# Three 256-column matmuls per weight tile in the transposed products, instead of one of 512 and one of 256 columns in two addends

## The chip, the cores and the metric

The kernel runs on one core of a Trainium2 chip. The metric is the device time of one execution in microseconds, taken from the first to the last instruction and what little lies around them. TensorE (PE) multiplies, ScalarE (ACT), VectorE (DVE) and GpSimd (POOL) do the rest, and SyncE (SP) issues the DMAs. PE has two kinds of rows in the trace: its matmuls (PE) and its weight loads (PEld), which run beside them.

## The reference

One decoder layer on 256 tokens of 2048 features: a SwiGLU half-step, a mixer of two branches (latent attention, MLA, and a gated linear recurrence, HGRN), and a second SwiGLU half-step, each between two RMS norms.

```python
def swiglu(h, w_gate, w_up, w_down):
    return (jax.nn.silu(h @ w_gate) * (h @ w_up)) @ w_down
...
    x = x + MACARON_SCALE * rmsnorm(swiglu(rmsnorm(x, ...), w_gate, w_up, w_down), ...)
    proj = rmsnorm(x, ...) @ w_in        # c_q, c_kv, k_rope, hq, hf, hi, hg, gate_a, gate_b
    y_a = mla_branch(c_q, c_kv, k_rope, positions, ...)
    y_b = hgrn2_branch(hq, hf, hi, hg, ...)
    merged = sigmoid(gate_a) * y_a + sigmoid(gate_b) * y_b
    x = x + rmsnorm(merged @ w_out, ...)
    x = x + MACARON_SCALE * rmsnorm(swiglu(rmsnorm(x, ...), ...), ...)
```

Everything is float32. The width of the FFN is 5632.

## The kernel before

Every product takes both operands as sums of two float32r parts, hi and lo, and adds up three of the four partial products: hi by hi, hi by lo, lo by hi. The weights arrive by DMA in tiles of 128 x 1024 (`raw`, four buffers). ACT casts the tile to its hi part (`whi`, L95) and DVE subtracts it to get the lo part (`wlo`, L96), with four buffers each; both run about one product ahead of PE. The activation is kept split as [128, part, k-tile, 256 tokens] (`h1`, `after1`, `h2`, `oa`, `ob`, `cqT`, `ckvT`; in the trace `h`, `after` and so on).

There are two kinds of products. `gemm_n` has the activation as the loaded operand and the weights as the moving one (L126 to L128), 512 columns at a time, or 256 in the value products of MLA (`w_v`). `gemm_t` has the weights as the loaded operand, 128 columns at a time, and the activation as the moving one; its result is transposed, [column, token]. It is called 144 times: 80 times in the two FFNs (gate and up), 16 for the mixer's gates, 16 for HGRN's q and f, 16 for the two output projections, and 16 times over four k-tiles only, for MLA's q and k; all others run over 16 k-tiles. For each k-tile and each half j of 256 weight columns it issues two matmuls into the bank of that half: lo against the first part of the activation (256 columns, L114), and hi against both parts side by side (512 columns, L115); at the first k-tile the one of 512 comes first (L111, L112), since it has to open the whole bank. So a bank holds two addends of 256 columns. `Ops.total` adds them: ACT copies one out (L120) and DVE adds the other (L121); `pair_in` of HGRN has a `total` of its own (L630, L631) that also reorders. What follows (Silu, Sigmoid, the products with the gates) reads the sum from SBUF; in the two output projections POOL multiplies by the gates (L360, L375).

A product of the rotary key (L477 to L479) has weights of 64 columns and is written apart: three matmuls of 256 columns each, hi with the first part, hi with the second, lo with the first, into one region.

PSUM has two buffers `mm` of two banks each, which products take in turn, two of `tp` and two of `sp`. The order on each engine is the order in which the program is written, with some chains put ahead by `high_priority` (AHEAD); PE issues its matmuls strictly in that order. In HGRN the matmuls of a scan (L728, L741, L754) stand between those of the following pair's products.

Of the kernel before, what the change touches and what calls it, by code (L numbers as in the profile page):

```python
# [9 lines left out]
F32 = mybir.dt.float32  # L10
# [4 lines left out]
ALU = mybir.AluOpType  # L15
# [4 lines left out]
P = 128  # L20
# [17 lines left out]
# Where the next operand's transposes stand in program order, along the product that runs beside them (see gemm_n), and  # L38
# by how many instructions the rest of that operand's chain is put ahead; columns of the residual at a time.
# [9 lines left out]
def _two_pi_parts():  # L49
    """2 pi as a sum of four 12-bit numbers and a rest."""  # L50
    parts, rest = [], TWO_PI
    for _ in range(4):
        step = 2.0 ** (np.floor(np.log2(rest)) - 11)
        c = np.floor(rest / step) * step
        parts.append(float(c))
        rest -= c
    parts.append(float(np.float32(rest)))
    return parts


class Ops:
    """Pools and the pieces that the stages share."""
# [36 lines left out]
    def gemm_t(self, w, act, kt):  # L99
        """256 weight columns, result transposed: a bank for 128 columns, [column, token] in two addends."""  # L100
        nc = self.nc
        ps = self.mm.tile([P, 2, 512], F32, name="mm")
        for g in range(kt // 4):
            hi, lo = self.load_w(w[g])
            for i in range(4):
                k = g * 4 + i
                for j in range(2):
                    c = slice(i * 256 + j * P, i * 256 + (j + 1) * P)
                    both = act(k)
                    if k == 0:  # L110
                        nc.tensor.matmul(ps[:, j], hi[:, c], both, start=True, stop=False)  # L111
                        nc.tensor.matmul(ps[:, j, 0:T], lo[:, c], both[:, 0], start=False, stop=False)  # L112
                    else:
                        nc.tensor.matmul(ps[:, j, 0:T], lo[:, c], both[:, 0], start=False, stop=False)  # L114
                        nc.tensor.matmul(ps[:, j], hi[:, c], both, start=False, stop=k == kt - 1)  # L115
        return ps

    def total(self, out, ps):
        """The sum of gemm_t's two addends."""
        self.nc.scalar.copy(out=out, in_=ps[:, :, T:512])  # L120
        self.nc.vector.tensor_tensor(out=out, in0=out, in1=ps[:, :, 0:T], op=ALU.add)  # L121
# [8 lines left out]
    def gemm_n(self, w, act, kt, n=512, late=0, pool=None, own=0, hooks=()):  # L130
        """n weight columns, result [token, column], a bank for each half of the tokens.

        The first half of the tokens ends its last `late` k-tiles before the second half starts them. Their
        weights are in `pool`, but for the first `own` tiles. `hooks` are functions to call at points that run
        from -1 to 0 along the first half of the tokens, and from 0 to 1 along the second's last k-tiles."""
# [36 lines left out]
    def rstd_of(self, ssq, n, width, half=False):  # L172
        """ssq [P, n] sums of squares -> 1 / sqrt(mean + eps), or half of it."""
# [20 lines left out]
    def transposed(self, src, act, c, tt):  # L194
        """split(transpose(src)) into the k-tiles 4c.. of act."""
# [10 lines left out]
    def prenorm(self, x, ssq, wname, act, tt, ws=None):  # L206
        """act = split(transpose(x * rstd * w)) for half of the tokens."""
# [10 lines left out]
    def weighted(self, ps, c, z, wname):  # L218
        """z = y * w, a quarter of the columns."""
# [3 lines left out]
    def residual(self, x, z, rstd, done):  # L223
        """x += rstd * z, some of the columns at a time."""
# [6 lines left out]
    def closing(self, w, act, kt, late, own, pool, post, half, x_src, x_dst, nxt):  # L231
        """The last product of a stage, its norm, the residual, and the next stage's operand.

        Returns the hooks of the next product, which end the operand."""
# [33 lines left out]
def layer_kernel(ctx, tc, a, out):  # L268
# [9 lines left out]
    def ffn(n, act, fp, x_src, x_dst, nxt, hooks=()):  # L278
# [3 lines left out]
        # the first columns by halves of the tokens  # L282
# [8 lines left out]
        for c in range((FF - FF_N) // 256):  # L291
            pg = ops.gemm_t(wg[c], act, KD)
            sg = fp.tile([P, 2, T], F32, name="sg", bufs=2)
            ops.total(sg, pg)
            S.activation(out=sg, in_=sg, func=AF.Silu)
            pu = ops.gemm_t(wu[c], act, KD)
            su = ops.small.tile([P, 2, T], F32, name="m", bufs=2)
            ops.total(su, pu)
            V.tensor_tensor(out=sg, in0=sg, in1=su, op=ALU.mult)
# [39 lines left out]
    def gate_a(c):  # L339
        pg = ops.gemm_t(a["w_ga"][c], h, KD)  # L340
        g = ga[:, 2 * c:2 * c + 2]
        ops.total(g, pg)
        S.activation(out=g, in_=g, func=AF.Sigmoid)

    def gate_b(c):
        pg = ops.gemm_t(a["w_gb"][c], h, KD)
        t = gbp.tile([P, 2, T], F32, name="gb", bufs=3)
        ops.total(t, pg)
        S.activation(out=t, in_=t, func=AF.Sigmoid)
# [5 lines left out]
    for c in range(8):  # L355
        py = ops.gemm_t(a["mla_w_o"][c], lambda k: oa[:, :, k, :], KD)
        m = ops.small.tile([P, 2, T], F32, name="m", bufs=2)
        ops.total(m, py)
        g = ga[:, 2 * c:2 * c + 2]
        G.tensor_tensor(out=g, in0=g, in1=m, op=ALU.mult)  # L360
# [5 lines left out]
    with tc.tile_pool(name="mg", bufs=1, side="right", reuse_waits="tile") as mgp:  # L366
        mg = mgp.tile([P, 2, KD, T], F32R, name="mg")
        for c in range(8):
# [5 lines left out]
            ops.total(m, py)  # L374
            G.tensor_tensor(out=m, in0=m, in1=gts[c], op=ALU.mult)  # L375
# [15 lines left out]
def rope_tables(ops, pool):  # L391
    """cos and sin of positions * inv_freq as [token, half of the tokens, HALF]."""
# [17 lines left out]
    # whole turns off: their number in parts of ten bits, so that each product with a part of 2 pi is exact  # L410
# [22 lines left out]
def mla(ops, mp, c_q, hm, h, oa, gate):  # L433
# [16 lines left out]
    def rope(dst, src, tt, n):  # L450
        """src [P, n, 64] -> dst, rotated."""
# [18 lines left out]
    # k_rope: product transposed, back to [token, dim], rotated, transposed, for the even and the odd  # L470
    # head of a pair in its half of the partitions, with zeros in the other
# [40 lines left out]
    def heads_in(pair, step):  # L512
        qn = mp.tile([P, 2, T], F32, name="qn", bufs=3)
        ops.total(qn, ops.gemm_t(a["w_q_nope"][pair], cq, KL))
        step()
        kn = mp.tile([P, 2, T], F32, name="kn", bufs=3)
        ops.total(kn, ops.gemm_t(a["w_k_nope"][pair], ckv, KL))
# [381 lines left out]
```

## Time and profile before

| what | us |
|---|---|
| median of three runs | 2564.39 (2564.3 to 2566.51) |
| span of the profiled execution | 2564.2 |
| PE busy | 2521.4 |
| PE weight loads busy | 2147.1 |
| DVE busy | 1477.7 |
| ACT busy | 1186.9 |
| POOL busy | 181.1 |

The span of the profiled execution is 0.2 us under the median; what lies around it is less than the runs differ by. PE's rows overlap each other, so the distance between the starts of two matmuls in a row tells more than the duration of one. In the 40 slices of the page PE is at 9 tenths or more but for the first and the last, the granted clock is at 9 or more throughout, and the DMA engines are busy between 4 and 8 tenths.

### The profile page before, as it was taken

To read this page: it belongs to the slowest core of one execution; us is meant where nothing else is said; L and a number is where in the kernel's file an instruction comes from. 1 tells how busy PE (TensorE), PEld (TensorE's weight loads), DVE (VectorE), ACT (ScalarE), POOL (GpSimd) and SP (SyncE) were. 2 spreads that over 40 slices of the span, in tenths; PEclk is the share of its full clock that TensorE was granted. 3 is DMA by queue.
4 is the path that set the end of the run, shared out by engine and by line. 5 is a ranking of instruction groups with operands and counts; after the bars stand their busy time and mean duration, and the time that the engine had idled before them with its cause. 6 is when DMAs were issued, how large, how long until landed. Compare 5 with 4: busy or idle time off the path is not lost.

```text
span 2564.2 us, 33907 instructions
## 1 busy us (share of the span) xinstructions
PE 2521.4 (98%) x13316; PEld 2147.1 (84%) x13316; DVE 1477.7 (58%) x1732; ACT 1186.9 (46%) x1552; POOL 181.1 (7%) x181
## 2 busy tenths in 40 slices
PE   8999999999999999999999999999999999999998
PEld 6888888888878898888888888888788888888887
DVE  5555555544466666556777776555655555554444
ACT  5444444434344556444444444444544444443433
POOL 0000000000000100111323231120000000000000
PEclk9999999999999999999999999999999999999999
DMA  7555555556686444555545444567755555555655
GB/s 255 174 188 189 188 183 190 188 188 199 201 271 188 162 140 148 188 181 181 165 163 169 161 157 158 188 205 242 231 175 188 187 186 188 189 189 188 197 195 184
DMA packets 137248, 481.13 MB, mean 188 GB/s; under 512 B 15616, under 2 KB 16000, under 8 KB 136320
## 3 DMA queue, kind: packets, MB, share of 16 engines
q1 hardware_dynamic: 137088, 478.97, 57.3%
q8 instruction: 104, 1.70, 0.3%
q14 instruction: 56, 0.46, 0.1%
HBM read 472.61 MB, written 6.29 MB: 187 GB/s over the span
## 4 chain that ended last, share of the span: by engine, by line
PE 93%; DVE 3%; POOL 1%; issue 1%; DMA 1%; ACT 1%; SPq 0%; POOLq 0%; DVEq 0%; ACTq 0%
PE mm L115 34%; PE mm L114 18%; PE mm L126 11%; PE mm L127 11%; PE mm L128 11%; PE mm L111 2%; PE mm L112 1%; POOL suf L706 1%; PE tp L198 0%; DVE sT L711 0%; PE sp L534 0%; PE sp L533 0%; DVE wlo L96 0%; PE sp L728 0%; PE tp L565 0%
## 5 line engine op out<-in xcount | busy, mean ns | idle before, releaser
L96 DVE TENSOR_TENSOR wlo<-raw,whi 128x1024 fp32r<-128x1024 f32 x826 | 1024.8, 1243 | 763.5 <-ACT whi L95 762.3
L95 ACT CAST whi<-raw 128x1024 fp32r<-128x1024 f32 x826 | 865.7, 1050 | 891.2 <-PE mm L115 425.3
L115 PE MATMUL mm<-h,whi 128*128 128x512 f32 x2400 | 846.0, 393 | 0.0
L114 PE MATMUL mm<-h,wlo 128*128 128x256 f32 x2400 | 678.1, 283 | 0.0
L115 PEld LDWEIGHTS mm<-h,whi 128*128 128x128 f32 x2400 | 450.7, 188 | 100.7
L114 PEld LDWEIGHTS mm<-h,wlo 128*128 128x128 f32 x2400 | 451.2, 188 | 3.8
L115 PE MATMUL mm<-after,whi 128*128 128x512 f32 x960 | 340.1, 394 | 0.0
L114 PE MATMUL mm<-after,wlo 128*128 128x256 f32 x960 | 273.1, 284 | 0.0
L127 PE MATMUL mm<-wlo,at 128*128 128x512 f32 x664 | 262.0, 395 | 0.0
L126 PE MATMUL mm<-whi,at 128*128 128x512 f32 x664 | 262.0, 395 | 0.0
L128 PE MATMUL mm<-whi,at 128*128 128x512 f32 x664 | 261.7, 395 | 0.0
L115 PEld LDWEIGHTS mm<-after,whi 128*128 128x128 f32 x960 | 180.4, 188 | 38.9
L114 PEld LDWEIGHTS mm<-after,wlo 128*128 128x128 f32 x960 | 180.6, 188 | 1.2
L126 PEld LDWEIGHTS mm<-whi,at 128*128 128x128 f32 x664 | 125.1, 188 | 29.2
L128 PEld LDWEIGHTS mm<-whi,at 128*128 128x128 f32 x664 | 125.1, 188 | 29.2
L127 PEld LDWEIGHTS mm<-wlo,at 128*128 128x128 f32 x664 | 125.1, 188 | 29.2
L178 POOL TENSOR_TENSOR rs<-ms,mhalf 128x1 f32<-128x1 f32 x16 | 9.7, 605 | 1633.3 <-DVE ms L176 1633.3
L126 PE MATMUL mm<-whi,after 128*128 128x512 f32 x304 | 120.9, 398 | 1.2 <-ACT after L164 1.2
L128 PE MATMUL mm<-whi,after 128*128 128x512 f32 x304 | 120.1, 395 | 0.0
L127 PE MATMUL mm<-wlo,after 128*128 128x512 f32 x304 | 120.0, 395 | 0.0
L115 PE MATMUL mm<-oa,whi 128*128 128x512 f32 x240 | 84.6, 393 | 0.0
L115 PE MATMUL mm<-ob,whi 128*128 128x512 f32 x240 | 84.6, 393 | 0.0
(276 smaller groups left out, 2860.9 us busy)
## 6 DMA issues: line engine op xcount, KB each, us to landing
raw<-in_ffn_w_gate SPq DMA_DIRECT2D x176, 512.0 KB, 4.3
raw<-in_ffn_w_up SPq DMA_DIRECT2D x176, 512.0 KB, 3.5
raw<-in_ffn_w_down SPq DMA_DIRECT2D x176, 512.0 KB, 4.3
raw<-in_w_ga SPq DMA_DIRECT2D x32, 512.0 KB, 3.4
raw<-in_mla_w_o SPq DMA_DIRECT2D x32, 512.0 KB, 3.6
raw<-in_w_hq SPq DMA_DIRECT2D x32, 512.0 KB, 3.6
raw<-in_w_hf SPq DMA_DIRECT2D x32, 512.0 KB, 3.5
raw<-in_w_hi SPq DMA_DIRECT2D x32, 512.0 KB, 3.5
```

The costliest lines, as they stand in the source:

```text
L95: nc.scalar.copy(out=hi, in_=raw)
L96: nc.vector.tensor_tensor(out=lo, in0=raw, in1=hi.bitcast(F32), op=ALU.subtract)
L111: nc.tensor.matmul(ps[:, j], hi[:, c], both, start=True, stop=False)
L112: nc.tensor.matmul(ps[:, j, 0:T], lo[:, c], both[:, 0], start=False, stop=False)
L114: nc.tensor.matmul(ps[:, j, 0:T], lo[:, c], both[:, 0], start=False, stop=False)
L115: nc.tensor.matmul(ps[:, j], hi[:, c], both, start=False, stop=k == kt - 1)
L126: nc.tensor.matmul(o, both[:, 0, r], hi[:, c], start=k == 0, stop=False)
L127: nc.tensor.matmul(o, both[:, 0, r], lo[:, c], start=False, stop=False)
L128: nc.tensor.matmul(o, both[:, 1, r], hi[:, c], start=False, stop=k == kt - 1)
L178: self.nc.gpsimd.tensor_tensor(out=r, in0=ms, in1=self.mhalf[:, 0:n], op=ALU.pow)
L706: G.tensor_tensor(out=part(suf, n, True), in0=part(suf, n, True), in1=ends(pre, n, False), op=ALU.mult)
```

## The change

`gemm_t` issues three matmuls of 256 columns for each k-tile and half, all into the first 256 columns of the bank: hi with the first part of the activation, hi with the second part, lo with the first part. The first opens the region at the first k-tile, the last closes it at the last. The result is complete in PSUM, and `total` is gone. Silu and Sigmoid on ACT and the multiplies on DVE read PSUM; MLA's q and k are copied out by ACT; in the two output projections the multiply by the gate moves from POOL to DVE, with its operand from PSUM; HGRN's q and f are read in the order that `total` made. Comments and docstrings are taken out, so that line numbers move.

```diff
     def gemm_t(self, w, act, kt):
-        ps = self.mm.tile([P, 2, 512], F32, name="mm")
+        banks = self.mm.tile([P, 2, 512], F32, name="mm")
+        ps = banks[:, :, 0:T]
...
                     both = act(k)
-                    if k == 0:
-                        nc.tensor.matmul(ps[:, j], hi[:, c], both, start=True, stop=False)
-                        nc.tensor.matmul(ps[:, j, 0:T], lo[:, c], both[:, 0], start=False, stop=False)
-                    else:
-                        nc.tensor.matmul(ps[:, j, 0:T], lo[:, c], both[:, 0], start=False, stop=False)
-                        nc.tensor.matmul(ps[:, j], hi[:, c], both, start=False, stop=k == kt - 1)
+                    nc.tensor.matmul(ps[:, j], hi[:, c], both[:, 0], start=k == 0, stop=False)
+                    nc.tensor.matmul(ps[:, j], hi[:, c], both[:, 1], start=False, stop=False)
+                    nc.tensor.matmul(ps[:, j], lo[:, c], both[:, 0], start=False, stop=k == kt - 1)
         return ps
-
-    def total(self, out, ps):
-        self.nc.scalar.copy(out=out, in_=ps[:, :, T:512])
-        self.nc.vector.tensor_tensor(out=out, in0=out, in1=ps[:, :, 0:T], op=ALU.add)
...
             sg = fp.tile([P, 2, T], F32, name="sg", bufs=2)
-            ops.total(sg, pg)
-            S.activation(out=sg, in_=sg, func=AF.Silu)
+            S.activation(out=sg, in_=pg, func=AF.Silu)
             pu = ops.gemm_t(wu[c], act, KD)
-            su = ops.small.tile([P, 2, T], F32, name="m", bufs=2)
-            ops.total(su, pu)
-            V.tensor_tensor(out=sg, in0=sg, in1=su, op=ALU.mult)
+            V.tensor_tensor(out=sg, in0=sg, in1=pu, op=ALU.mult)
...
         py = ops.gemm_t(a["mla_w_o"][c], lambda k: oa[:, :, k, :], KD)
-        m = ops.small.tile([P, 2, T], F32, name="m", bufs=2)
-        ops.total(m, py)
         g = ga[:, 2 * c:2 * c + 2]
-        G.tensor_tensor(out=g, in0=g, in1=m, op=ALU.mult)
+        V.tensor_tensor(out=g, in0=g, in1=py, op=ALU.mult)
...
         qn = mp.tile([P, 2, T], F32, name="qn", bufs=3)
-        ops.total(qn, ops.gemm_t(a["w_q_nope"][pair], cq, KL))
+        S.copy(out=qn, in_=ops.gemm_t(a["w_q_nope"][pair], cq, KL))
...
-        total(q, ops.gemm_t(a["w_hq"][pr], h, KD))
-        S.activation(out=sg, in_=q, func=AF.Sigmoid)
-        V.tensor_tensor(out=q, in0=q, in1=sg, op=ALU.mult)
+        pq = ordered(ops.gemm_t(a["w_hq"][pr], h, KD))
+        S.activation(out=sg, in_=pq, func=AF.Sigmoid)
+        V.tensor_tensor(out=q, in0=sg, in1=pq, op=ALU.mult)
```

The gates, HGRN's f and the second output projection change in the same way.

On PE, at the turn from one FFN product to the next (`mm` with its number is the product's PSUM buffer, `h1` the activation, `whi` and `wlo` the two parts of a weight tile), before:

```order
L114 MATMUL mm_804<-h1_86,wlo_874 128x256
L115 MATMUL mm_804<-h1_86,whi_873 128x512
L111 MATMUL mm_899<-h1_86,whi_902 128x512
L112 MATMUL mm_899<-h1_86,wlo_903 128x256
L111 MATMUL mm_899<-h1_86,whi_902 128x512
L112 MATMUL mm_899<-h1_86,wlo_903 128x256
L114 MATMUL mm_899<-h1_86,wlo_903 128x256
L115 MATMUL mm_899<-h1_86,whi_902 128x512
```

The same place on PE in the changed kernel:

```order
L111 MATMUL mm_893<-h1_86,whi_986 128x256
L112 MATMUL mm_893<-h1_86,whi_986 128x256
L113 MATMUL mm_893<-h1_86,wlo_987 128x256
L111 MATMUL mm_1017<-h1_86,whi_1020 128x256
L112 MATMUL mm_1017<-h1_86,whi_1020 128x256
L113 MATMUL mm_1017<-h1_86,wlo_1021 128x256
```

Each pair of rows has become three, and the special order of the first k-tile is gone; between other work the triples stand where the pairs stood, within a matmul or two.

On DVE, over one gate and one up product of an FFN (`sg` is the gate, `m` the sum of the up product, `at` the split result), before:

```order
L165 TENSOR_TENSOR at<-sg,at 128x512
L96 TENSOR_TENSOR wlo<-raw,whi 128x1024 x3
L121 TENSOR_TENSOR sg<-sg,mm 128x512
L96 TENSOR_TENSOR wlo<-raw,whi 128x1024 x4
L121 TENSOR_TENSOR m<-m,mm 128x512
L299 TENSOR_TENSOR sg<-sg,m 128x512
L96 TENSOR_TENSOR wlo<-raw,whi 128x1024
L165 TENSOR_TENSOR at<-sg,at 128x512
```

The same stretch of DVE in the changed kernel:

```order
L158 TENSOR_TENSOR at<-sg,at 128x512
L96 TENSOR_TENSOR wlo<-raw,whi 128x1024 x7
L289 TENSOR_TENSOR sg<-sg,mm 128x512
L96 TENSOR_TENSOR wlo<-raw,whi 128x1024
L158 TENSOR_TENSOR at<-sg,at 128x512
```

The add for the gate has gone from between the splits of weights, and the multiply (L299, now L289; L165 is now L158) takes its second operand from PSUM.

## Rows read from the trace of the kernel before

**Rows 1.** The page's part 1: engine, busy us, share of the span, instructions.

```profile
PE 2521.4 (98%) x13316; PEld 2147.1 (84%) x13316; DVE 1477.7 (58%) x1732; ACT 1186.9 (46%) x1552; POOL 181.1 (7%) x181
```

**Rows 2.** The page's part 4: the chain that ended last.

```profile
PE 93%; DVE 3%; POOL 1%; issue 1%; DMA 1%; ACT 1%; SPq 0%; POOLq 0%; DVEq 0%; ACTq 0%
PE mm L115 34%; PE mm L114 18%; PE mm L126 11%; PE mm L127 11%; PE mm L128 11%; PE mm L111 2%; PE mm L112 1%; POOL suf L706 1%; PE tp L198 0%; DVE sT L711 0%; PE sp L534 0%; PE sp L533 0%; DVE wlo L96 0%; PE sp L728 0%; PE tp L565 0%
```

**Rows 3.** By stage: us, busy (count) of PE, PEld, DVE, ACT, POOL; clock; DMA.

```profile
70.00:515.00 445.00, 445.00 (x2537) 389.63 (x2536) 243.91 (x236) 207.27 (x237) 0.00 (x0) 1.00 0.58 187
515.00:750.00 235.00, 235.00 (x1014) 190.65 (x1013) 111.23 (x97) 95.28 (x102) 0.00 (x0) 1.00 0.65 210
...
1205.00:1560.00 355.00, 342.83 (x1852) 289.62 (x1851) 259.60 (x406) 167.31 (x300) 108.43 (x108) 1.00 0.49 157
```

**Rows 4.** Timeline of PE, steady FFN product: start us, duration us, engine, line, operation.

```profile
505.26 0.28 PE L114 MATMUL mm<-h,wlo 128*128 128x256 f32 x1
505.38 0.39 PE L115 MATMUL mm<-h,whi 128*128 128x512 f32 x1
505.60 0.28 PE L114 MATMUL mm<-h,wlo 128*128 128x256 f32 x1
505.72 0.40 PE L115 MATMUL mm<-h,whi 128*128 128x512 f32 x1
...
511.22 0.28 PE L114 MATMUL mm<-h,wlo 128*128 128x256 f32 x1
```

**Rows 5.** Timeline of PE, a value product of MLA.

```profile
873.79 0.28 PE L126 MATMUL mm<-whi,ckvT 128*128 128x256 f32 x1
873.90 0.28 PE L127 MATMUL mm<-wlo,ckvT 128*128 128x256 f32 x1
...
876.40 0.28 PE L128 MATMUL mm<-whi,ckvT 128*128 128x256 f32 x1
```

**Rows 6.** Timeline of PE, the product of the rotary key.

```profile
817.06 0.28 PE L477 MATMUL mm<-after,whi 128*64 128x256 f32 x1
817.18 0.28 PE L478 MATMUL mm<-after,whi 128*64 128x256 f32 x1
...
818.46 0.28 PE L477 MATMUL mm<-after,whi 128*64 128x256 f32 x1
```

**Rows 7.** Timeline of PE, the head of an FFN product.

```profile
504.09 0.28 PE L112 MATMUL mm<-h,wlo 128*128 128x256 f32 x1
504.21 0.28 PE L114 MATMUL mm<-h,wlo 128*128 128x256 f32 x1
504.32 0.39 PE L115 MATMUL mm<-h,whi 128*128 128x512 f32 x1
```

**Rows 8.** Timeline of PE, end of the last down product.

```profile
2549.74 0.39 PE L126 MATMUL mm<-wpair,at 128*128 128x512 f32 x1
...
2552.46 0.39 PE L126 MATMUL mm<-wpair,at 128*128 128x512 f32 x1
```

**Rows 9.** Weight loads by shape: line, operation, shapes, count, busy us, mean ns.

```profile
L115 PEld LDWEIGHTS mm<-h,whi 128*128 128x128 f32 x2400 | 450.7, 188 | 100.7
L477 PEld LDWEIGHTS mm<-after,whi 128*64 128x64 f32 x16 | 2.1, 134 | 0.0
```

**Rows 10.** Lines L120 and L121: count, duration in ns (least, median, most).

```profile
L120 ACT COPY m<-mm x56: 587/587/588, 88.1 to 2310.9; 128x512 f32<-128x512 f32 x56
L121 DVE TENSOR_TENSOR m<-m,mm x56: 686/687/690, 88.7 to 2311.6; 128x512 f32<-128x512 f32 x56
```

**Rows 11.** Timelines of PE and DVE in HGRN.

```profile
1216.92 0.68 PE L741 MATMUL sp<-A,B 128*128 128x128 f32 x4 [1.41 <-DVE B L737]
...
1228.12 0.69 DVE L631 TENSOR_TENSOR q<-q,mm 128x512 f32<-128x512 f32 x1 [0.52 <-ACT q L630]
```

**Rows 12.** Timeline of DVE, and the chain, at HGRN's last pair.

```profile
1548.71 0.68 DVE L121 TENSOR_TENSOR gb<-gb,mm 128x512 f32<-128x512 f32 x1
...
1549.39 1.05 ACT whi L95
```

More of the change, by code (lines that the diff above doesn't have):

```diff
@@ L341, in gate_a @@
         g = ga[:, 2 * c:2 * c + 2]
-        ops.total(g, pg)
-        S.activation(out=g, in_=g, func=AF.Sigmoid)
+        S.activation(out=g, in_=pg, func=AF.Sigmoid)
     def gate_b(c):
@@ L347, in gate_b @@
         t = gbp.tile([P, 2, T], F32, name="gb", bufs=3)
-        ops.total(t, pg)
-        S.activation(out=t, in_=t, func=AF.Sigmoid)
+        S.activation(out=t, in_=pg, func=AF.Sigmoid)
         return t
@@ L373, in layer_kernel @@
             cs = slice(2 * c, 2 * c + 2)
-            ops.total(m, py)
-            G.tensor_tensor(out=m, in0=m, in1=gts[c], op=ALU.mult)
+            V.tensor_tensor(out=m, in0=gts[c], in1=py, op=ALU.mult)
             G.tensor_tensor(out=m, in0=m, in1=ga[:, cs], op=ALU.add)
@@ L513, in heads_in @@
         qn = mp.tile([P, 2, T], F32, name="qn", bufs=3)
-        ops.total(qn, ops.gemm_t(a["w_q_nope"][pair], cq, KL))
+        S.copy(out=qn, in_=ops.gemm_t(a["w_q_nope"][pair], cq, KL))
         step()
         kn = mp.tile([P, 2, T], F32, name="kn", bufs=3)
-        ops.total(kn, ops.gemm_t(a["w_k_nope"][pair], ckv, KL))
+        S.copy(out=kn, in_=ops.gemm_t(a["w_k_nope"][pair], ckv, KL))
         step()
@@ L625, in pair_in, with ordered @@
         tmp = lambda: gp.tile([P, 2, 2, P], F32, name="tmp", bufs=2)
-        def total(t, ps):
-            o = t.rearrange("p t j n -> p j t n")
-            half = lambda s: ps[:, :, s * T:(s + 1) * T].rearrange("p j (t n) -> p j t n", n=P)
-            S.copy(out=o, in_=half(1))
-            V.tensor_tensor(out=o, in0=o, in1=half(0), op=ALU.add)
+        def ordered(ps):
+            return ps.rearrange("p j (t n) -> p t j n", n=P)
         q = gp.tile([P, 2, 2, P], F32, name="q", bufs=2)
         sg = tmp()
-        total(q, ops.gemm_t(a["w_hq"][pr], h, KD))
-        S.activation(out=sg, in_=q, func=AF.Sigmoid)
-        V.tensor_tensor(out=q, in0=q, in1=sg, op=ALU.mult)
+        pq = ordered(ops.gemm_t(a["w_hq"][pr], h, KD))
+        S.activation(out=sg, in_=pq, func=AF.Sigmoid)
+        V.tensor_tensor(out=q, in0=sg, in1=pq, op=ALU.mult)
         f = gp.tile([P, 2, 2, P], F32, name="f", bufs=2)
@@ L640, in pair_in @@
         step(1)
-        total(sf, ops.gemm_t(a["w_hf"][pr], h, KD))
+        pf = ordered(ops.gemm_t(a["w_hf"][pr], h, KD))
         step(1)
-        S.activation(out=sf, in_=sf, func=AF.Sigmoid)
+        S.activation(out=sf, in_=pf, func=AF.Sigmoid)
         for j in range(2):
```

## Prediction

> **What bounds the kernel now.** I read the page first: PE is busy 98% of the span, DVE 58%, ACT 46% [rows 1]. The chain that ended last is PE for 93%, and gemm_t's four lines (L111, L112, L114, L115) are 55% of the span on it; DVE, POOL and ACT together are 5% [rows 2]. The table by stage then says where PE waits at all: in the first FFN's transposed products PE is busy 445.00 of 445 us, in the down product 235.00 of 235, and only in the HGRN stage does it stand still, for 355 - 342.83 = 12 us. The granted clock is 1.00, the 2.4 GHz level, in each [rows 3]. So the end is set by how fast PE passes through its own queue of matmuls; time is lost or won per matmul slot, which I take as the distance from one start to the next. A row's own duration (0.28 us for 256 columns) is of no use for that, since matmuls overlap.
>
> In the steady part of an FFN product the pattern is one 256-column slot of 0.12 us and one 512-column slot of 0.22 us or a little more. From 505.26 to 511.22 there are 17 such pairs, so a pair takes 5.96 / 17 = 0.3506 us [rows 4]. A product over 16 k-tiles has 32 pairs and there are 128 of them; 16 products over 4 k-tiles have 8 pairs each: 4096 + 128 = 4224 pairs. They take 4224 x 0.3506 = 1481 us of 2564.2.
>
> **The change part by part.** *The matmuls.* Each pair becomes three slots of 256 columns. The columns are the same 768, so nothing is gained or lost by counting columns; what counts is what a third matmul, with a third weight load, adds. Break-even is a mean slot of 0.3506 / 3 = 0.1169 us. No row of before shows three full-width 256-column matmuls in a row with the activation moving, so I bound the slot from both sides.
>
> Below: the value products (w_v) stream 256 columns against 128-column loads, 23 slots from 873.79 to 876.40, 2.61 / 23 = 0.1135 us each [rows 5]. There the roles are swapped: the weights move and the activation is loaded. Three such slots are 0.3405, 0.0101 less than a pair, or 4224 x 0.0101 = 43 us less. In the middle: k_rope is already written as the changed code is, same moving operand and same order of hi, hi, lo, but loads only 64 weight columns; 12 slots from 817.06 to 818.46 are 1.40 / 12 = 0.1167 us [rows 6]. Three are 0.3500, 4224 x 0.0006 = 2.5 us less. Above: L114 is itself the third matmul of the changed triple, unaltered: lo against the first half of the activation, 256 columns, 128-column loads on both sides, into the same region. Its slot is 0.12 us [rows 4] (of the 17 in that stretch 15 read 0.12 and two 0.13, rounded as they are; I take 0.1200); three such are 0.3600, 0.0094 more than a pair, 4224 x 0.0094 = +39.7 us. I take this row, because it is the nearest: operands, widths and role are those of the new code, and the other two rows each differ in what is loaded. Against it stands one place: at the head of each product L112 is followed by L114, two 256-column matmuls in a row, and the two slots are 504.32 - 504.09 = 0.23 us together, 0.115 each [rows 7]. That is two slots in a transition; I keep it for the rivals.
>
> What would make the third slot cost something: a 512-column slot is 0.3506 - 0.1200 = 0.2306 us, a 256-column slot 0.1200; a straight line through the two gives 0.0094 us per matmul beside its columns. One matmul more per pair is then the same +39.7 us. But a second line, through the slots where the weights move, does not have that part: 512 columns take 2.72 / 12 = 0.2267 us from 2549.74 to 2552.46 [rows 8], which is twice 0.1135 to within 0.0003. So the price of a matmul as such is between 0 and 0.0094 us here, and which of the two holds decides the case.
>
> The Trainium skill (TensorE: Matmul & The Clock Gate, section Back-to-back issue gap) speaks against the change too: at the high clock it gives N / 2.4 ns plus a fixed 2.5 ns for each matmul. By that price the sum would be 4224 x 2.5 ns = +10.6 us, an estimate from that page. No row here shows a price of that size; the two lines give nothing and nearly four times as much.
>
> *The weight loads.* 4224 more. A load is recorded as 188 ns for 128 columns and 134 ns for 64 [rows 9], so 64 columns cost 54 ns and 128 about 108 ns of streaming (an estimate from these rows), the rest being latency. 108 ns fits under a slot of 113 to 120 ns, and the loads run beside the matmul before them; w_v shows exactly this load at that pace. They cost nothing by themselves, but they leave 5 to 12 ns of slack where a 512-column matmul left over 110; if that cover is gone, each slot is set by its load.
>
> *The totals.* 128 copies on ACT of 0.587 us fall away (75 us), and on DVE 144 adds of 0.687 us, while 16 multiplies by the gates come to DVE from POOL [rows 10]: 128 x 0.687 = 88 us less. None of it is on the path in the FFN stages, where PE waits for nobody [rows 3]. In HGRN the PE stalls belong to the scan: PE is held until 1216.92 by DVE's L737, and the chain there is POOL and DVE work on suf and f; the adds of the totals lie outside, at 1228.12 [rows 11]. The last pair has an add at 1548.71 just ahead of a step of the scan, 0.68 us, but ACT's cast of 1549.39 to 1550.44 ends after it on the chain [rows 12]. I take 0 of the 0.7 us. PSUM regions are released earlier by the two operations, and no PE row in the steady part waits for one: 0.
>
> *Order and waits.* On DVE the gate's add no longer stands between the splits, and the multiply by the up product waits for PE directly instead of for ACT's copy. Queued behind it are the next splits of weights (L96), which already stood behind the add that waited for the same product; they run one product ahead (4 buffers), and no PE time hangs on it in these stages. 0. With slower slots the scan's stalls shrink a little, since the products between its steps last longer: in each of 8 pairs some 5 us of such products by 2.7%, about -1 us in all.
>
> Sum: 2564.2 + 39.7 - 1 = 2602.9. The span of the profiled execution is 0.2 us under the median of 2564.39, so I predict **2603** us. Its own range is 2596 to 2609 (slots of 0.1195 to 0.1205: 33 to 46 us).
>
> **The rivals.** *The weight load sets the pace and the stream closes up (faster).* In w_v the slots are at 0.11 us from the first one on and stay at 0.1135. If the triples do the same, whichever operand is loaded, PE gains 43 us and gives about 1 us back in the scan's stalls: 2522. For it: the only long stream of this exact shape in the trace does so, and the pair at a product's head is at 0.115 [rows 5, 7]. Against it: L114, with the loads of the new code, never shows it in the steady part. It decides below a mean slot of 0.1169 us.
>
> *Splitting the 512 costs nothing (no change).* The halves take what the whole took, and the mean slot stays near k_rope's 0.1167: 2564.2 - 2.5 - 0.5 = 2561, between 2557 and 2568 for slots of 0.1164 to 0.1172 [rows 6]. For it: same operands and order. Against it: half the load.
>
> *A small fixed price per matmul.* The two straight lines give 0 and 0.0094 us; a price of a quarter of the second, 0.0025, adds 4224 x 0.0025 = 10.6 us: 2575. The page named above gives the same. Neither line supports the middle, so the chance is small.
>
> **How the numbers follow.** Forecast 0.42, closed-up stream 0.25, nothing 0.25, small price 0.08. The likeliest time is 2603. To leave out no more than 2 in 10 the range must reach both 2522 and 2603 with their spreads: 2520 to 2609. What a measurement here can tell from no change is about 0.2%, 5.1 us. Faster by more than that: the closed-up stream and 0.07 of the case of no change, 0.32. Within: 0.17. Slower: 0.42 + 0.08 + 0.01 = 0.51.
>
> **What would show it.** In the profile after, take the starts of the three lines in a steady FFN product: a triple of 0.360 us confirms the forecast, 0.350 the case of no change, 0.340 the closed-up stream; times 4224 it must give the difference in the end to a few us. The FFN stages should carry 80/144 of the products and a like share of the difference, PE's busy share there should stay whole, and ACT and DVE should lose some 75 and 88 us. If the triple is 0.350 and the time still moves by more than 5 us, then the consumers matter and my reading of what is off the path is wrong; the HGRN stage, with its 12 us of standing still, is where that would show. If PE begins to wait for splits or for PSUM in the FFN stages, the part on order is wrong.

## The result, and the profile after

The changed kernel takes 2590.34 us (median of 4, 2589.65 to 2594.64), the kernel before, run beside it, 2565.45 us (2564.30 to 2568.03): 24.9 us more, ratio 1.0099, interval [1.0084, 1.0113]. It is slower, as forecast; the forecast of 2603 us was 13 us too high.

The profiled execution of the changed kernel took 2594.64 us, its span 2592.9 us. Part 1 of its page (engine, busy us, share, instructions), and the chain that ended last:

```profile
PE 2549.6 (98%) x17540; PEld 2362.0 (91%) x17540; DVE 1386.2 (53%) x1604; ACT 1120.6 (43%) x1424; POOL 144.5 (6%) x165
```

```profile
PE 94%; DVE 3%; POOL 1%; issue 1%; DMA 1%; ACT 0%; SPq 0%; POOLq 0%; DVEq 0%; ACTq 0%
```

Beside [rows 1, 2]: 4224 matmuls and as many loads more, DVE 91 us less, ACT 66 and POOL 37 us less, and PE on the path as before. The weight loads went from 84% of the span to 91%. The same three stretches of time as in [rows 3], of which the second and third stage now begin later, by 12 and 17 us (us; busy us and count of PE, PEld, DVE, ACT, POOL; clock; DMA share; GB/s):

```profile
70.00:515.00 445.00, 445.00 (x3711) 445.00 (x3710) 214.04 (x193) 181.38 (x193) 0.00 (x0) 1.00 0.55 183
515.00:750.00 235.00, 235.00 (x1059) 192.51 (x1058) 109.91 (x94) 94.63 (x100) 0.00 (x0) 1.00 0.62 204
1205.00:1560.00 355.00, 342.37 (x2212) 308.41 (x2211) 246.64 (x376) 157.26 (x267) 102.61 (x109) 1.00 0.50 161
```

PE still waits for nobody in the FFN; in HGRN it stands still 355 - 342.37 = 12.6 us, against 12.2 before. What changed is that in the first stage a weight load is now under way at every moment: 445.00 of 445 us, where it was 389.63. No new wait was made and none removed. The time went into the slots. In the steady part of the first FFN (start us, duration us, engine, line, operation):

```profile
505.03 0.28 PE L113 MATMUL mm<-h,wlo 128*128 128x256 f32 x1
505.15 0.29 PE L111 MATMUL mm<-h,whi 128*128 128x256 f32 x1
505.27 0.28 PE L112 MATMUL mm<-h,whi 128*128 128x256 f32 x1
...
506.59 0.29 PE L111 MATMUL mm<-h,whi 128*128 128x256 f32 x1
```

From the first to the last are 13 slots, 1.56 / 13 = 0.1200 us each: every matmul of the triple goes at the pace that only L114 had in [rows 4]. A finer measure of the mean is how many matmuls pass in 300 us of a pure FFN product. Of the kernel before, and of the changed one (stretch, length, busy us of PE and count, clock, DMA share, GB/s):

```profile
100.00:400.00 300.00, 300.00 (x1711) 1.00 0.58 188
1950.00:2250.00 300.00, 300.00 (x1712) 1.00 0.58 187
```

```profile
100.00:400.00 300.00, 300.00 (x2502) 1.00 0.55 183
1950.00:2250.00 300.00, 300.00 (x2530) 1.00 0.57 186
```

Before, a pair takes 600 / 1711 = 0.3507 us in the first FFN and the same in the second. After, a triple takes 900 / 2502 = 0.3597 us in the first and 900 / 2530 = 0.3557 in the second, with the same instructions at the same addresses. (A count is good to about two, 0.0003 us of a triple and 0.0004 of a pair; paces with a count beside them are made this way below.) The mixer pays the second price: on `oa` 256 pairs took 89.9 us and 256 triples take 91.2, 0.0050 more each. With the first price for the 1280 triples of the first FFN and the second for the other 2944, the difference is 1280 x 0.0090 + 2944 x 0.0050 = 26 us; the spans of the two profiled executions differ by 28.7. The three executions without a profile have spans of 2587.8 to 2588.7 us, 4 to 5 us shorter. That is what the first FFN would give back at the second's pace (1280 x 0.0040 = 5.1), but no trace of them says so.

### The profile page after: what moved, and what is told of

The parts are those of the page before. It is cut to its first block, busy times and chain, and to the rows that moved or that the text cites. A ratio compares the mean times of both kernels' runs of the same rounds, so it can differ in the third digit from the quotient of the medians.

```text
span 2592.9 us, 42076 instructions
## 1 busy us (share of the span) xinstructions
PE 2549.6 (98%) x17540; PEld 2362.0 (91%) x17540; DVE 1386.2 (53%) x1604; ACT 1120.6 (43%) x1424; POOL 144.5 (6%) x165
## 4 chain that ended last, share of the span: by engine, by line
PE 94%; DVE 3%; POOL 1%; issue 1%; DMA 1%; ACT 0%; SPq 0%; POOLq 0%; DVEq 0%; ACTq 0%
PE mm L112 19%; PE mm L111 19%; PE mm L113 19%; PE mm L120 11%; PE mm L119 11%; PE mm L121 11%; POOL suf L688 1%; PE tp L191 1%; DVE sT L693 0%; PE sp L519 0%; PE sp L518 0%; PE tp L550 0%; PE sp L710 0%; ACT junk L163 0%; DVE wlo L96 0%
## 5 line engine op out<-in xcount | busy, mean ns | idle before, releaser
L111 PE MATMUL mm<-h,whi 128*128 128x256 f32 x2560 | 724.8, 283 | 0.0
L112 PE MATMUL mm<-h,whi 128*128 128x256 f32 x2560 | 724.8, 283 | 0.0
L113 PE MATMUL mm<-h,wlo 128*128 128x256 f32 x2560 | 724.7, 283 | 0.0
L112 PEld LDWEIGHTS mm<-h,whi 128*128 128x128 f32 x2560 | 484.6, 189 | 0.0
L113 PEld LDWEIGHTS mm<-h,wlo 128*128 128x128 f32 x2560 | 484.6, 189 | 0.0
L111 PEld LDWEIGHTS mm<-h,whi 128*128 128x128 f32 x2560 | 484.6, 189 | 0.0
L111 PE MATMUL mm<-after,whi 128*128 128x256 f32 x1024 | 292.0, 285 | 0.0
L112 PE MATMUL mm<-after,whi 128*128 128x256 f32 x1024 | 289.8, 283 | 0.0
L113 PE MATMUL mm<-after,wlo 128*128 128x256 f32 x1024 | 288.9, 282 | 0.0
L120 PE MATMUL mm<-wlo,at 128*128 128x512 f32 x664 | 262.0, 395 | 0.0
L121 PE MATMUL mm<-whi,at 128*128 128x512 f32 x664 | 261.7, 395 | 0.0
L112 PEld LDWEIGHTS mm<-after,whi 128*128 128x128 f32 x1024 | 193.0, 189 | 0.2
L111 PEld LDWEIGHTS mm<-after,whi 128*128 128x128 f32 x1024 | 193.0, 188 | 0.2
L113 PEld LDWEIGHTS mm<-after,wlo 128*128 128x128 f32 x1024 | 193.0, 188 | 0.0
L120 PEld LDWEIGHTS mm<-wlo,at 128*128 128x128 f32 x664 | 125.0, 188 | 29.4
L121 PEld LDWEIGHTS mm<-whi,at 128*128 128x128 f32 x664 | 125.0, 188 | 29.2
L121 PE MATMUL mm<-whi,after 128*128 128x512 f32 x304 | 120.1, 395 | 0.0
```

The costliest lines, as they stand in the source:

```text
L111: nc.tensor.matmul(ps[:, j], hi[:, c], both[:, 0], start=k == 0, stop=False)
L112: nc.tensor.matmul(ps[:, j], hi[:, c], both[:, 1], start=False, stop=False)
L113: nc.tensor.matmul(ps[:, j], lo[:, c], both[:, 0], start=False, stop=k == kt - 1)
L120: nc.tensor.matmul(o, both[:, 0, r], lo[:, c], start=False, stop=False)
L121: nc.tensor.matmul(o, both[:, 1, r], hi[:, c], start=False, stop=k == kt - 1)
```

## Experiments

Four theories. **1**: the third matmul with its weight load costs, because a load takes nearly as long as 256 columns. **2**: the columns set the pace. **3**: the addresses of the loaded and the streamed operand set it. **4**: the consumers, or the loss of the sum, made the difference.

### The third matmul or the consumers

*One part alone: the split, with the sum and all consumers of before.*

```diff
...
-  nc.tensor.matmul(ps[:, j], hi[:, c], both, start=False, stop=k == kt - 1)
+  nc.tensor.matmul(ps[:, j, 0:T], hi[:, c], both[:, 0], start=False, stop=False)
+  nc.tensor.matmul(ps[:, j, T:512], hi[:, c], both[:, 1], start=False, stop=k == kt - 1)
```

> The kernel before, with each 512-column matmul of the transposed products split into two of 256 columns into the same two addends; the vector engine's sum of the addends and every consumer stay as before. If the third matmul is what costs (theory 1), this one is as slow as the changed kernel: triples of about 0.357 us instead of pairs of 0.351, 2590 us, between 2580 and 2595. If the consumers that now read PSUM, or the loss of the sum, cost the time (theory 4), it stays at 2565 us.

Measured: 2597.35 us (2590.52 to 2599.09), ratio 1.0115 [1.0098, 1.0132]. Its counts in the two stretches are those of the changed kernel, to one:

```profile
100.00:400.00 300.00, 300.00 (x2503) 1.00 0.53 183
1950.00:2250.00 300.00, 300.00 (x2531) 1.00 0.54 186
```

So the split alone makes the whole loss; its median is 2 us above the range expected. The triple is slow also where its halves go into two regions of PSUM.

*The other part alone: pairs of 512 and 256 columns, consumers reading PSUM, no sum; the second addend is computed and left out of the result.*

```diff
-  nc.tensor.matmul(ps[:, j], hi[:, c], both[:, 0], start=k == 0, stop=False)
-  nc.tensor.matmul(ps[:, j], hi[:, c], both[:, 1], start=False, stop=False)
-  nc.tensor.matmul(ps[:, j], lo[:, c], both[:, 0], start=False, stop=k == kt - 1)
...
+  nc.tensor.matmul(banks[:, j, 0:T], lo[:, c], both[:, 0], start=False, stop=False)
+  nc.tensor.matmul(banks[:, j], hi[:, c], both, start=False, stop=k == kt - 1)
```

> The changed kernel with the pairs of 512 and 256 columns of the kernel before: its consumers read the first addend in PSUM, and the second addend, one of three partial products, is left out, as is the sum. If the third matmul makes the whole difference (theory 1), the time is that of the kernel before, 2565 us within 0.2%. If the consumers that read PSUM cost time (theory 4) it lies above that, up to 2590 us; if the loss of the sum gains time, below 2560 us.

Measured: 2564.83 us, ratio 0.9994 [0.9985, 1.0004]: -1.5 us, between -3.8 and +1.0. Its first stretch:

```profile
100.00:400.00 300.00, 300.00 (x1711) 1.00 0.53 188
```

The pace of before, and the time of before, without 128 copies on ACT and, on balance, 88 us of work on DVE. They were off the path, and so is what replaced them. Theory 4 falls.

### What a slot is made of

*Half the columns of the second product: 128 of the 256 tokens of hi by the low part are left out.*

```diff
-  nc.tensor.matmul(ps[:, j], hi[:, c], both[:, 1], start=False, stop=False)
+  nc.tensor.matmul(ps[:, j, 0:P], hi[:, c], both[:, 1, 0:P], start=False, stop=False)
```

> The changed kernel, whose second product of each triple (weight high part by activation low part) streams only 128 of the 256 tokens; half of one partial product is left out. If a slot is paced by the weight load that goes with it (theory 1), this slot stays at 0.113 us or more and the time falls by less than 25 us, to 2565 or more. If it is paced by its columns (theory 2), the slot falls to about 0.06 us, 4224 of them give back some 220 us, and the time is near 2370 us.

Measured: 2568.99 us (2567.10 to 2571.52), 21 us below the changed kernel, not 220. The timeline of PE in the first FFN, the weight loads at the same place (first and last of seven), and the count:

```profile
449.84 0.28 PE L111 MATMUL mm<-h,whi 128*128 128x256 f32 x1
449.96 0.22 PE L112 MATMUL mm<-h,whi 128*128 128x128 f32 x1
450.02 0.33 PE L113 MATMUL mm<-h,wlo 128*128 128x256 f32 x1
450.19 0.28 PE L111 MATMUL mm<-h,whi 128*128 128x256 f32 x1
...
451.58 0.28 PE L111 MATMUL mm<-h,whi 128*128 128x256 f32 x1
```

```profile
449.73 0.19 PEld L111 LDWEIGHTS mm<-h,whi 128*128 128x128 f32 x1
...
450.42 0.19 PEld L111 LDWEIGHTS mm<-h,whi 128*128 128x128 f32 x1
```

```profile
100.00:400.00 300.00, 300.00 (x2598) 1.00 0.56 190
```

Both expectations on the slot were half right. The half stream does take only 0.06 us, but what it saves the next slot gives back: 0.17 us from 450.02 to 450.19 for a matmul of 0.12. Removing a sixth of the columns made a triple 900 / 2598 = 0.3464 us, a gain of 0.009 to 0.013. The loads do not follow the uneven slots: from 449.73 to 450.42 they start 0.10 to 0.12 us apart, 0.115 on the mean. So something that comes three times in a triple and does not shorten with the stream keeps the pace. The time fell by less than the triples say, since the mixer gave some of it back: the FFNs' products on h are 17 and 12 us shorter than in the changed kernel, but from the first product on `oa` to the first on `ob` it takes 9 us more, with PE standing still for 24 us there instead of 13 and the granted clock at 0.97 in two stretches of 100 us.

*All three matmuls stream 128 tokens, but for each product's first triple; half of the transposed products is left out.*

```diff
-  both = act(k)
-  nc.tensor.matmul(ps[:, j], hi[:, c], both[:, 0], start=k == 0, stop=False)
...
+  both, n = act(k), T if k == 0 else P
+  nc.tensor.matmul(ps[:, j, 0:n], hi[:, c], both[:, 0, 0:n], start=k == 0, stop=False)
...
```

> The changed kernel, with all three matmuls of a triple streaming 128 of the 256 tokens, but for the first triple of each product; half of the work of the transposed products is left out. If the three weight loads pace a triple (theory 1, 0.1156 us a load by the sum of the three slots with one half stream), it still takes 0.346 us: some 4224 times 0.011 us less than the changed kernel, 2545 us, between 2530 and 2565. If its columns do, the three slots are 0.060 us each as the half stream's slot was, and the time is under 2000 us.

Measured: 2602.25 us (2599.20 and 2605.30), more than the changed kernel with twice the columns. In the first FFN:

```profile
449.84 0.27 PE L112 MATMUL mm<-h,whi 128*128 128x128 f32 x1
...
451.18 0.27 PE L112 MATMUL mm<-h,whi 128*128 128x128 f32 x1
```

```profile
100.00:400.00 300.00, 300.00 (x2677) 1.00 0.57 196
```

Twelve slots in 1.34 us, 0.112 each, where a slot of 128 columns took 0.06 in the run before; a triple is 900 / 2677 = 0.336 us, below the 0.346 expected. I read 0.112 as the pace of 128-column weight loads one behind the other, the only thing left that takes so long. The Trainium skill (TensorE: Matmul & The Clock Gate, section LDWEIGHTS (loading the stationary operand)) gives a load as its columns divided by 1.2, in ns, by which an estimate for 128 is 107 ns. These slots are 5 ns above that. Theory 2 falls, and load and stream are seen apart: 0.112 us for a load, 0.1133 for 256 columns, half a slot of [rows 8]. In the changed kernel the slot with both is longer than either, 0.117 to 0.120; in [rows 5] it is not, at 0.1135. The time, expected at 2545, went elsewhere: in the HGRN stage the granted clock fell.

```profile
1100.00:1200.00 100.00, 97.26 (x661) 1.00 0.55 185
1200.00:1300.00 100.00, 96.91 (x559) 0.80 0.38 132
...
1500.00:1600.00 100.00, 92.81 (x507) 0.78 0.35 121
```

```profile
1210.00:1220.00 10.00, 10.00 (x48) 0.50 0.30 107
```

The last row, 10 us with 0.50, is the 1.2 GHz level. The mean clock of this kernel's two executions is 0.966 and 0.963; the kernel with half of one stream, above, has 0.993 to 0.996, and all others 0.997 to 0.999. It differs from the changed kernel, whose clock is 1.00 in all of HGRN, in that PE streamed half as many columns before and between the scan's stalls. The FFNs' products on h are 30 and 25 us shorter than in the changed kernel, and from the first product on `oa` to the first on `ob` it takes 63 us more: what was gained in the FFN was lost there.

*The third matmul loads 64 of its 128 weight columns; half of one partial product is left out.*

```diff
+  q = slice(c.start, c.start + (P if k == kt - 1 else 64))
-  nc.tensor.matmul(ps[:, j], lo[:, c], both[:, 0], start=False, stop=k == kt - 1)
+  nc.tensor.matmul(ps[0:q.stop - q.start, j], lo[:, q], both[:, 0], start=False, stop=k == kt - 1)
```

> The changed kernel, whose third matmul of a triple (low part of the weights) loads and computes 64 of its 128 weight columns, but for the last triple of a product; it streams the same 256 tokens, and half of one partial product is left out. If the loads pace the triple (theory 1), a load that is 0.054 us shorter brings it down to its three streams, 0.340 to 0.350 us, and the time to 2520 to 2560 us. If each matmul has a price of its own whatever it loads, the triple stays at 0.357 us and the time at 2590 us.

Measured: 2578.84 us (2578.11 to 2579.81), 11.5 us below the changed kernel. The weight loads (count, busy us, mean ns) and the first stretch:

```profile
L112 PEld LDWEIGHTS mm<-h,whi 128*128 128x128 f32 x2560 | 480.5, 188 | 0.0
L114 PEld LDWEIGHTS mm<-h,wlo 128*64 128x64 f32 x2400 | 322.7, 134 | 0.0
```

```profile
100.00:400.00 300.00, 300.00 (x2551) 1.00 0.53 187
```

A triple takes 900 / 2551 = 0.3528 us, 0.003 to 0.007 less than with three full loads, with the same count of matmuls and as many streamed columns. Time and triple lie between the two expectations. The loads do cost, so theory 1 is right in its direction; but a load shorter by 0.054 us gave back at most 0.007, and all three slots still read 0.11 to 0.13 us. It is not the sum of the loads that a triple waits for.

*The two halves of the weight columns in turn, so that no two matmuls in a row add into the same region.*

```diff
-  nc.tensor.matmul(ps[:, j], hi[:, c], both[:, 0], start=k == 0, stop=False)
...
+  for j in range(2):
+      nc.tensor.matmul(ps[:, j], hi[:, cs[j]], both[:, 0], start=k == 0, stop=False)
+  for j in range(2):
+      nc.tensor.matmul(ps[:, j], hi[:, cs[j]], both[:, 1], start=False, stop=False)
...
```

> The changed kernel with the two halves of the 256 weight columns taken in turn, so that no two matmuls in a row add into the same region of PSUM or use the same weight columns; the count of matmuls and loads is the same. If adding three times in a row into one region is what slows the slots, they fall to 0.1133 us and the time to 2520 to 2560 us. If the loads pace them (theory 1), 2590 us within 0.2%.

Measured: 2593.41 us (2591.89 to 2594.43), ratio 1.0105 [1.0090, 1.0120]: as slow as the changed kernel. Its count, the same in both FFNs:

```profile
100.00:400.00 300.00, 300.00 (x2530) 1.00 0.54 185
```

That is 0.3557 us a triple, the changed kernel's pace in its second FFN. Adding into one region is not the cause.

### Where the operands lie

In the built programs the weight tiles `whi` and `wlo` begin 160 bytes past a multiple of 512, the operand tiles of the FFN and the two output projections 288 bytes past one, and so do the tiles `wpair`, which hold the weights of the last k-tiles of some `gemm_n` products. An unused tile ahead of them moves the tiles at 288 (and MLA's `cqT` and `ckvT`, at 224), leaves `whi` and `wlo` where they are, and changes nothing else on TensorE:

```diff
+  self.pad = self.hp.tile([P, 96], F32, name="pad")      # 384 bytes; 32 for 128, 64 for 256, 16 for 64
+  self.nc.gpsimd.memset(self.pad, 0.0)
```

*384 bytes, in the kernel before and in the changed one.*

> The kernel before, with an unused tile of 384 bytes a partition ahead of the activation tiles, so that activations lie at the same offset modulo 512 bytes as the weight tiles; no instruction on TensorE changes. If the offset between the loaded and the streamed operand sets the pace of the slots (theory 3), the 512-column slots fall from 0.231 to 0.227 us and the 256-column ones from 0.120 to 0.1133, and the time to about 2500 to 2535 us. If the offset has nothing to do with it, 2565 us within 0.2%.

> The changed kernel with the same unused tile of 384 bytes. If the offset sets the pace (theory 3), the three slots of a triple fall to 0.1133 us each, 0.340 a triple, and the time to about 2500 to 2525 us. If not, 2590 us within 0.2%.

Measured: the kernel before comes to 2552.80 us, ratio 0.9948 [0.9933, 0.9963]; the changed one to 2587.95 us (2587.42 to 2588.81), ratio to the kernel before 1.0086 [1.0071, 1.0101]. Counts in an FFN product and in the down product (600 to 740 us), first of the kernel before as it was:

```profile
600.00:740.00 140.00, 140.00 (x604) 1.00 0.65 214
```

then of the kernel before with 384 bytes:

```profile
100.00:400.00 300.00, 300.00 (x1703) 1.00 0.54 187
600.00:740.00 140.00, 140.00 (x619) 1.00 0.65 221
```

and of the changed kernel with 384 bytes:

```profile
100.00:400.00 300.00, 300.00 (x2502) 1.00 0.53 183
1950.00:2250.00 300.00, 300.00 (x2502) 1.00 0.53 183
600.00:740.00 140.00, 140.00 (x620) 1.00 0.63 215
```

The 512-column slot of the down product falls from 140 / 604 = 0.232 us to 140 / 619 = 0.226, the pace of [rows 8], so theory 3 holds there. The pair does not follow: 600 / 1703 = 0.3523, longer by 0.0016. And the triple, which was to fall to 0.340, stands at 0.3597 in both FFNs; the changed kernel's time is the one expected if the offset does nothing. At these addresses the third matmul costs 0.3597 - 0.3523 = 0.0074 us a pair. Both effects are in the 13 us that the kernel before gains.

*128 and 256 bytes, in the kernel before.*

> The kernel before with an unused tile of 128 bytes a partition ahead of the activation tiles: streamed and loaded operand of every product are then 256 bytes apart modulo 512. If their distance sets the pace of a slot (theory 3, refined: distance 0 gave 0.2267 us for a 512-column slot of the down products against 0.2324 us, and 0.353 us against 0.351 us for the pairs), these slots move again, and the time lies outside 2560 to 2570 us. If only a distance of 0 is special, 2565 us within 0.2%.

> The same with 256 bytes: the streamed operand lies 384 bytes after the loaded one modulo 512 in the down products (128 in the kernel before) and 128 in the transposed products (384 in the kernel before). If the distance sets the pace, the down products' slots come to what the transposed products' 512-column slots had at that distance, 0.2306 us, and the time changes by under 10 us; if it does not, 2565 us within 0.2%.

Measured: 2555.30 us, ratio 0.9955 [0.9940, 0.9970], and 2565.83 us, ratio 1.0001 [0.9992, 1.0010]. Counts with 128 bytes, then with 256:

```profile
100.00:400.00 300.00, 300.00 (x1703) 1.00 0.54 186
600.00:740.00 140.00, 140.00 (x619) 1.00 0.64 221
```

```profile
100.00:400.00 300.00, 300.00 (x1712) 1.00 0.55 188
600.00:740.00 140.00, 140.00 (x605) 1.00 0.62 214
```

128 bytes give the counts of 384, and 256 those of no pad. With these four pads the pace goes by the distance of loaded and streamed operand modulo 256 bytes: 0 (pads of 384 and 128) makes down products' slots 0.226 us and pairs 0.3523; 128 (no pad, and 256) makes them 0.232 and 0.3507. That it is the distance and not the operand's own place shows in the kernel before: with `at` at the same address, slots with `whi` and `wlo` take 0.232 us, slots with `wpair`, at distance 0, take 0.2267 [rows 8]. The expectation for 256 bytes named 0.2306 us for the down product's slot; it kept 0.231 to 0.232.

*The offsets chosen by product: operands of the FFN's transposed products at 128, those of the down products at 0.*

```diff
-  t = ops.hp.tile([P, 2, KD, T], F32R, name=name, tag="H")
+  room, at = ops.hp.tile([P, 2 * KD * T + 96], F32R, name=name, tag="H"), 96 if name[0] == "a" else 0
+  t = room[:, at:at + 2 * KD * T].rearrange("p (s k t) -> p s k t", s=2, k=KD)
```

> The kernel before, with 384 spare bytes in the operand tile: the operands of the FFN products that are transposed (h1, h2) stay at their offset, after1 and all tiles behind it come to the offset of the weights. If the offset sets the pace (theory 3), the pairs on h1 and h2 keep 0.351 us and the down products' 512-column slots take 0.2267 us: some 5 us less than with the tile of 384 bytes ahead of all of them, 2547 us, between 2542 and 2551. If not, 2553 us or more.

Measured: 2551.66 us (2550.53 to 2553.61), ratio 0.9947 [0.9934, 0.9959].

```profile
100.00:400.00 300.00, 300.00 (x1711) 1.00 0.54 187
600.00:740.00 140.00, 140.00 (x619) 1.00 0.64 222
```

Both paces came out as said, but the time is at the upper end: 1.1 us less than with 384 bytes ahead of everything, not 5. The expectation counted the pairs on h1 and h2 (2560 x 0.0016 = 4 us) and left out the 512-column slots in which h1 and h2 are loaded and the weights move; there are 384 of them, and in steady rows they go from 0.2267 us with 384 bytes ahead of everything to 0.2324, some 2 us. The rest is no more than the spread of its runs. This is the fastest kernel of the study, 14 us under the kernel before, with no instruction of TensorE changed; it is not told apart from the one with 384 bytes.

*64 bytes, in the changed kernel.*

> The changed kernel with an unused tile of 64 bytes a partition ahead of the activation tiles: in the transposed products the loaded operand then lies 64 bytes after the streamed one modulo 256, in the down products 192. In the run with 384 bytes the few triples on cqT stood at 64 and their three slots took 0.117 us (some 0.113) against 0.119 at 192; 512-column slots at 192 took 0.229 us. If the third matmul's price is a matter of these offsets, triples fall to about 0.350 us and down products' slots to 0.229, and the time to about 2550 us (2540 to 2565). If it is the loads whatever the offset, the triples stay at 0.356 us or more and the time is 2575 to 2590 us.

Measured: 2563.97 us, ratio 0.9981 [0.9962, 1.0001], no longer slower than the kernel before. But ten executions run from 2541.64 to 2569.49 us, all at clock 0.998 to 0.999, a spread that no other kernel here had. The profiled execution, of 2564.82 us, has several paces side by side. The first FFN, the product on oa, and the down product:

```profile
100.00:400.00 300.00, 300.00 (x2550) 1.00 0.54 186
1040.00:1110.00 70.00, 70.00 (x620) 1.00 0.56 191
600.00:740.00 140.00, 140.00 (x604) 1.00 0.61 211
```

```profile
1079.85 0.28 PE L114 MATMUL mm<-oa,whi 128*128 128x256 f32 x1
...
1081.21 0.28 PE L114 MATMUL mm<-oa,whi 128*128 128x256 f32 x1
```

On h a triple takes 900 / 2550 = 0.3529 us. On oa, at the same distance of 64 bytes, 12 slots take 1.36 us, 0.1133 each, which is 0.340 for a triple: the closed-up stream of the first rival, with three full loads. The products on `ob` do the same, 96 triples in 32.64 us. So three full loads do not force a slot of 0.12, and since h, oa and ob lie at the same place, neither does the distance alone. The same code runs at one of several steady paces, as the two FFNs of the changed kernel do at 0.3597 and 0.3557. The down product, which was to fall to 0.229 us a slot, stayed at 140 / 604 = 0.232; products of HGRN's values and gates, at the same distance of 192, ran at 0.229 to 0.230.

## Why the prediction was right

**What bounds the kernel: right.** PE's queue set the end before and after; no wait appeared in the FFN stages, and PE's standing still in HGRN stayed at some 12 us.

**The price of the third matmul: right in mechanism, too large in size.** The forecast took L114's slot for all three, 0.3600 a triple, +0.0094 a pair. The first FFN gave just that, 0.3597 and +0.0090. The other stages gave +0.0050, which was not among the rows of before. Instead of 39.7 us it is 26 by the two prices, and 24.9 by the medians. The step that was too coarse is the one that made one row stand for 4224 triples.

**The range: in part luck.** 2590.34 lies between the forecast's own range, 2596 to 2609, and the small price at 2575. It is inside 2520 to 2609 because that range had to reach down to the closed-up stream, which did not come. Of the signs named in advance, 0.360 for a triple came in one of two FFNs; the other's 0.3557 belongs to none. The share expected of the FFN stages, 80/144, counts products; by pairs it is 2560 / 4224 = 61%, and their products grew by 12 and 7 us of the 28.7 between the two spans.

**The straight lines: both wrong as laws.** A price per matmul of 0 or of 0.0094 us was read from two kinds of slot and taken for a property of the shape. Part of the difference between these two kinds was their addresses: with the operands moved, the down product's slots went from 0.232 to 0.226 us. That could have been seen before: [rows 8] is the end of a down product that elsewhere ran at 140 / 604 = 0.232 us a slot, so its 0.2267 was the exception. Nor are the rows constants of their lines. The value products and the rotary key are the same code at the same addresses after as before, yet most of them changed. Two stretches of the changed kernel, to set beside [rows 5] and [rows 6]:

```profile
924.01 0.28 PE L120 MATMUL mm<-wlo,ckvT 128*128 128x256 f32 x1
...
926.60 0.28 PE L121 MATMUL mm<-whi,ckvT 128*128 128x256 f32 x1
```

```profile
825.46 0.28 PE L462 MATMUL mm<-after,whi 128*64 128x256 f32 x1
...
827.26 0.28 PE L462 MATMUL mm<-after,whi 128*64 128x256 f32 x1
```

The first is 22 slots in 2.59 us, 0.1177 each, where 0.1135 stood before; six of the eight value products are like it, and the first two still take 0.1135. The second is 15 slots in 1.80 us, 0.1200, where 0.1167 stood; the rotary key's next stretch, from 828.68, is at 0.1167 again. The rival bounds of 0.1135 and 0.1167 a slot were states of a stream, and so was the 0.1200 that was taken.

**The weight loads: right in part.** "If that cover is gone, each slot is set by its load" holds for short streams: three of 128 columns still take three loads' time, 0.112 us each. With 256 columns the load has a part, since a shorter third load shortens the triple, but it does not set the slot: slots of 0.117 to 0.120 us are longer than the load, half a load less gave back at most 0.007 us of a triple, and with 64 bytes of pad three full loads ran at 0.340. What the forecast lacked is that load and stream, each under 0.114, mostly make 0.117 to 0.120 together.

**Totals, consumers, order: right.** They were put at 0 to -1 us; the run with the consumers alone gave -1.5 [-3.8, +1.0]. DVE lost 91 us for 88 expected, ACT 66 for 75, and neither mattered.

**The rivals.** The closed-up stream (2522 us) did not come in the changed kernel, but it exists: with 64 bytes of pad it runs on oa. No change (2561) falls with the result, and with the run of the split alone. The small price of 0.0025 us (2575) is half of what the cheaper stages paid and under a third of the first FFN's. The Trainium skill (TensorE: Matmul & The Clock Gate, section Back-to-back issue gap) has 2.5 ns a matmul, by which the estimate was the same 2575, but states it for a single matmul apart; of streams of loads and matmuls it says that both set the spacing. The runs with short streams and with a short load bear the second out.

**What stays open.** Why a stream settles into one pace and not the next, how load and stream together come to 0.117 to 0.120 us, and why 512-column slots and pairs want opposite distances, no run here tells. The kernel before with 64 bytes of pad was not run, so the change is not shown to be free at that address: with 384 bytes in both, it costs 2587.95 - 2552.80 = 35 us.

## What to carry to other kernels

Where a 128-column load and 256 streamed columns take nearly the same time (0.112 and 0.1135 us here), a wide matmul is cover for the loads around it: cutting it in two cost 0.005 to 0.009 us a cut at the addresses of these two kernels, and freeing engines that nobody waited for paid none of it back. Before a pace is taken from a row, look for the same shape in two stages; if they differ, the row is a state and belongs in the range, not in the sum. When PE's queue is the bound, try where its operands lie: a pad of 128 or 384 bytes was worth 10 to 13 us here, about half of what the change cost.

## What the runs showed of the hardware

- Distance of loaded and streamed operand modulo 256 bytes: at 0 a 512-column slot of the down product takes 0.226 us and a pair 0.3523; at 128 they take 0.232 and 0.3507. Pads of 128 and 384 bytes agree, and so do 0 and 256. At 64 and 192 no single pace holds: triples of 0.353 and 0.340, 512-column slots of 0.229 and 0.232.
- The same instructions at the same addresses run at different steady paces: triples of 0.3597 and 0.3557 us in the two FFNs of one execution, 0.353 and 0.340 on h and on oa with 64 bytes of pad, where ten executions span 28 us.
- A matmul of 128 columns with its 128-column load takes 0.112 us in a stream of its kind, but 0.06 us between wider ones, when the next slot stretches to 0.17 and the loads keep starting 0.115 us apart.
- With half the columns in the transposed products, the granted clock in HGRN fell to 0.78 and 0.80 in two stretches of 100 us and to 0.50 in one of 10 us, with PE recorded as busy for 93 and 97% of them, and a kernel with less work took 2602 us.
